# A two-layer-path hybrid mixer step on one core: head sums of the recurrence in runs of five, and an earlier flag that holds back the modulation columns

## The chip, the core and the metric

The kernel runs on one core of one Trainium2 chip. The metric is the time of one execution on the device in microseconds; the medians below are medians of the runs shown. The engines are named as in the profile: PE (matmuls) with PEld (its weight loads), DVE, ACT, POOL, and SP, which only issues transfers.

## What is computed

The reference computes one layer of a diffusion backbone for two groups of tokens: 128 context tokens (`xp`) and 512 latent tokens (`xs`), 640 in all, with 1024 channels. Cut to what matters here:

```python
def trunk_layer(x, cvec, lw, ...):
    mod = jax.nn.silu(cvec) @ lw['w_ada'] + lw['b_ada']        # modulation: six rows of 1024 per group
    sh1, sc1, g1, sh2, sc2, g2 = jnp.split(mod, 6, axis=-1)
    h = rmsnorm(x, lw['norm1_g']) * (1.0 + sc1) + sh1
    mix, ... = token_mixers(h, lw, ...)                        # four gated mixers
    x = x + g1 * mix
    h = rmsnorm(x, lw['norm2_g']) * (1.0 + sc2) + sh2
    x = x + g2 * conv_ffn(h, lw['w_up'], ..., lw['w_down'])

def token_mixers(h, lw, ...):
    proj = h @ lw['w_in']                                      # 13 sections
    y_a = a_b * dwconv3(a_c * a_x, ...)
    y_b, s_f, s_b = hgrn2_bidir(b_q, b_ff, b_fb, b_i, b_g, ...)   # the recurrence, both directions
    y_c = neighbourhood_attention(...)                         # or context_attention
    y_d = chunk_gmlp(d_u, d_v, ...)
    g_a, g_b, g_c, g_d = split(sigmoid(h @ w_gate + b_gate))
    merged = g_a * (y_a @ w_br_a) + g_b * (y_b @ w_br_b) + g_c * (...) + g_d * (...)
    return merged @ lw['w_o'], ...
```

In the recurrence, each of 4 heads of 64 channels has a 64x64 state that decays and is updated along the tokens, forward and backward; the output of a head is normalised by the root mean square of its 64 values (`o * rsqrt(mean(o*o) + EPS)`), scaled and gated.

## The kernel before

Activations lie with channels on the 128 partitions and the 640 tokens along the free dimension, split in a high and a low part (`XH`, `XL`), as is each weight block (`w`, 128x1280 or 128x1024 for each part), so that a product takes three passes of `g` or `m` matmuls. A **main stream** runs through a list of weight blocks: the sections of `w_in` (line 362 inside `gemm_half`, and 933 for two sections with tokens on the partitions), then the gate and branch blocks (still line 362), then the output, up and down products. A block is loaded by SP into a `raw` tile, ACT copies its high part into `w` (lines 310, 323, 148), and the low part is made by DVE (line 324, and 311) or, for some blocks, by a transfer that POOL issues and that accumulates onto `w` (line 148, `w<-raw`).

Beside the main stream run **generators**: `ada_cols` (line 241, modulation columns), `hgrn` (line 445, the recurrence), `gmlp`, `conva`, `attn` (line 729, attention), `g_operands` (line 1011). The main stream counts planned microseconds: each step calls `tick(us)`, which adds to `now` and resumes every generator whose due time has passed; a generator that yields `x` is due again after `x` times its slack (1.3 for `hgrn`). `pe(us)` adds to `now` without resuming any. So the yields set the order in which instructions are written, and a scheduler then fixes the order of each engine from it. The engines work through their orders one instruction at a time.

What the change touches:

- `along(x)` (lines 459 to 469) sums a product of two 128x1280 tiles along the heads: ten matmuls of a 128x128 block with `heads` (128x2, ones for each head's partitions), into one PSUM tile `m`. It is called twice, on tile D and on tile E.
- The tail of `hgrn` (lines 611 to 655). For five blocks of 128 tokens the output `og` is copied out of PSUM, squared (ACT), summed over 64 (line 635, DVE, into `hss`), scaled (line 304, DVE), raised to the power -0.5 (line 305, POOL), and multiplied on (line 610, DVE, `normed`). The product of one block is written behind the sums of the next. Then comes a pause, the last `normed`, the flag `hgrn_y`, a pause `HY` of 4, and five times two transposes (line 648, PE) with their multiply (line 652, DVE). At the end `split_y("D", sg)` and `split_y("E", yt)` (lines 662, 663: a copy by ACT, a subtraction by DVE).
- `ada_cols` makes a modulation column in two halves on DVE: `junk<-H` (or A), then `H<-H` in place (both line 262, 128x1024), each with the sum of its row, and a small `modt` (line 228 or 231). The weights of even columns are loaded to region H, of odd ones to X0 or A, by SP (line 248); the load of column f+2 is written behind the second half of column f. While `hgrn_y` is set and `hgrn_done` is not, it starts no further column.

Two consumers stand behind these on the same engines. The attention works by units: scores on PE (lines 827, 830), bias and maximum on DVE (834, 836), exponential on ACT (837), reciprocal and scaling on DVE (843, 844), three transposes on PE (847), a copy of them to B by DVE (1931) or ACT (1929), the product with the values on PE (864), and its split by ACT and DVE (870, 871). The gate blocks end in a sigmoid on ACT (971; the first one behind the exponentials loads another table), which frees a PSUM tile `g`. Later blocks are of another kind, whose weights `raw` are combined in region H first (line 148, `H<-raw` by ACT, then sums by DVE).

Of the kernel before, what the change touches and what calls it, by code (L numbers as in the profile page):

```python
# [67 lines left out]
def tile_step(ctx: ExitStack, tc: tile.TileContext, a: dict, outs: list, dbg=None):  # L68
# [21 lines left out]
    def pe(us):  # L90
        now[0] += us
# [38 lines left out]
    def pm():  # L130
        return psm.tile([P, 512], F32, tag="m", name=nm("m"))
# [74 lines left out]
    for x in LORD.split():  # L206
        if x[0] == "w":
            i, h = int(x[1]), int(x[2])
# [170 lines left out]
    R = {}  # L379
# [67 lines left out]
    def hgrn():  # L447
# [13 lines left out]
        def along(x):  # L461

            m = pm()
            mv = m[:, 0:20].rearrange("p (r i) -> p i r", r=2)
            for i in range(10):
                mm(mv[:, i, :], x[:, i * P:(i + 1) * P], heads, start=True, stop=True)
                pe(0.22)
                yield 0.5
            return m


# [5 lines left out]
        for j in range(2):  # L477
            vec.tensor_tensor(n2[:, j], k2(j)[:, j], q2(1 - j)[:, 1 - j], ALU.mult)
        dm = yield from along(ksum)

        near_at = hd[:, 1280:1920].rearrange("p (r i t) -> p r i t", r=2, i=10)
# [17 lines left out]
        for l in range(7):  # L499
# [5 lines left out]
            if l == 0:  # L505
                m = yield from along(near)
                vec.copy_predicated(nat, lmask[:, 0, :].unsqueeze(1).to_broadcast([P, 20, 32]), bc(m))
# [101 lines left out]
        def normed(t):  # L609
            vec.tensor_tensor(o3(og, t), o3(og, t), ss[:, 4 * t:4 * t + 4].unsqueeze(2).to_broadcast([P, 4, 64]),  # L610
                              ALU.mult)
# [26 lines left out]
                normed(last)  # L638
            last = t
        R["hgrn_out"] = True  # L640
        yield 2.5
        normed(last)
        R["hgrn_y"] = True
        yield HY
        for t in range(5):
            m = pm()
# [251 lines left out]

    SLACK = {"q": 1.3, "du": 1.4, "ax": 1.0, "cv": 1.1}
    starts = {"q": hgrn, "du": gmlp, "ax": conva, "cv": attn}  # L900

    def in_tile(sec, n, w):
# [1318 lines left out]
```

## Time and profile before

| what | us |
|---|---|
| runs shown | 3496.3, 1024.87, 1024.14 |
| median | 1024.87 |
| the profiled execution's own time | 1023.97 |
| its span in the trace | 1022.1 |
| PE busy, of the span | 1008.3 (99%) |
| DVE busy | 790.1 (77%) |
| ACT busy | 538.6 (53%) |

The granted TensorE clock was 0.998 in the profiled execution. In a row of a timeline stand the start, the duration, the engine, the line, the operation, the tile written and the tiles read, and the number of instructions; brackets behind it give the idle time of the engine just before and what ended it. A tile's name is that of its buffer or region. "DMA to landing" is the time from a load's issue to its arrival. PE's ends are modelled, so starts are compared. A busy PE with an idle gap that has a releaser is a wait; idle time of another engine costs nothing by itself.

### The profile page before, as it was taken

Reading aid. Unit: us, or ns where it says so; the run is one execution under the profiler, and the core shown is the slowest. Engines: PE = TensorE matmul, PEld = TensorE weight load, DVE = VectorE, ACT = ScalarE, POOL = GpSimd, SP = SyncE. Lnnn points to the kernel's source line nnn. Section 1 sums busy time; section 2 is a strip of 40 time slices with the busy share of each in tenths; the row PEclk is TensorE's granted clock in tenths of the full one; section 3 lists DMA queues with packets and bytes.
Section 4 is the critical chain, followed back from the end, with each engine's and each line's share of the span. In section 5 each row is a group of like instructions: output and inputs, shape, how many; then the busy total and the mean of one; then the engine's idle time right before and its main releaser. Section 6 shows DMA issues by size and latency. Waiting matters only on the chain.

```text
span 1022.1 us, 18764 instructions
## 1 busy us (share of the span) xinstructions
PE 1008.3 (99%) x7572; PEld 951.9 (93%) x7572; DVE 790.1 (77%) x1308; ACT 538.6 (53%) x933; POOL 106.5 (10%) x153
## 2 busy tenths in 40 slices
PE   8999999999999999999999999999999999999997
PEld 6899999999899999999998899999999999888886
DVE  6758899769866676767868879998888887796644
ACT  6642343354555444444544567777777776634432
POOL 1000020312100000000010111111112221001101
PEclk9999999999999999999999999999999999999999
DMA  9864433597562413323179584765555669974212
GB/s 354 322 221 127 126 124 114 171 263 216 143 206 79 155 52 104 130 77 104 49 282 349 207 328 112 195 163 150 150 151 149 154 161 271 370 259 146 83 42 103
DMA packets 55926, 177.85 MB, mean 174 GB/s; under 512 B 8192, under 2 KB 14624, under 8 KB 53280
## 3 DMA queue, kind: packets, MB, share of 16 engines
q1 hardware_dynamic: 45008, 140.60, 39.6%
q0 software_dynamic: 10832, 36.06, 14.8%
q8 instruction: 59, 0.97, 0.4%
q14 instruction: 27, 0.22, 0.1%
HBM read 134.93 MB, written 25.46 MB: 157 GB/s over the span
## 4 chain that ended last, share of the span: by engine, by line
PE 91%; DVE 5%; DMA 1%; issue 1%; ACT 1%; POOL 1%; SPq 0%; POOLq 0%; DVEq 0%; ACTq 0%
PE g L1478 19%; PE m L1122 17%; PE g L362 14%; PE g L1813 8%; PE m L1813 6%; PE g L1135 5%; PE m L1478 4%; PE m L1262 3%; PE g L933 2%; PE g L1262 2%; PE m L148 2%; PE g L148 1%; PE m L1473 1%; PE m L526 1%; DMA A<-in_w_ada_dram 1%
## 5 line engine op out<-in xcount | busy, mean ns | idle before, releaser
L362 PE MATMUL g<-XH,w 128*128 128x320 f32 x704 | 171.4, 317 | 0.0
L362 PEld LDWEIGHTS g<-XH,w 128*128 128x128 f32 x704 | 120.6, 188 | 2.4 <-issue 1.2
L362 PE MATMUL g<-XL,w 128*128 128x320 f32 x352 | 108.8, 309 | 0.0
L362 PEld LDWEIGHTS g<-XL,w 128*128 128x128 f32 x352 | 66.3, 188 | 0.0
L311 DVE TENSOR_TENSOR w<-raw,w 128x1024 fp32r<-128x1024 f32 x34 | 41.4, 1221 | 14.9 <-ACT w L310 9.1
L1122 PE MATMUL m<-XH,w 128*128 128x320 f32 x224 | 52.5, 309 | 0.0
L1813 PE MATMUL g<-w,XH 128*128 128x512 f32 (+1 forms) x216 | 50.2, 385 | 0.0
L1813 PEld LDWEIGHTS g<-w,XH 128*128 128x128 f32 x216 | 39.5, 188 | 8.3 <-ACT XH L1772 0.3
L310 ACT ACTIVATE w<-raw 128x1024 fp32r<-128x1024 f32 x34 | 35.7, 1050 | 21.3 <-PE g L1262 10.0
L1813 PE MATMUL g<-w,XL 128*128 128x512 f32 (+1 forms) x180 | 42.4, 386 | 0.0
L148 DVE SCALAR_TENSOR_TENSOR X<-MG,p2t,X 128x641 f32<-128x641 f32 x44 | 38.9, 885 | 4.3 <-ACT X L148 3.4
L148 DVE SCALAR_TENSOR_TENSOR X<-X,p2t,X 128x641 f32<-128x641 f32 x44 | 38.9, 884 | 1.9 <-ACT X L148 1.0
L1813 PEld LDWEIGHTS g<-w,XL 128*128 128x128 f32 x180 | 33.4, 188 | 7.1 <-DVE dt L1828 0.2
L148 ACT ACTIVATE w<-raw 128x1024 fp32r<-128x1024 f32 (+3 forms) x46 | 38.2, 851 | 2.7 <-DMA raw<-in_w_in_dram 1.7
L1478 PE MATMUL g<-XL,w 128*128 128x320 f32 x240 | 38.6, 310 | 0.0
L1478 PE MATMUL g<-XL,C 128*128 128x320 f32 x240 | 38.4, 309 | 0.0
L1122 PEld LDWEIGHTS m<-XH,w 128*128 128x128 f32 x224 | 38.3, 188 | 0.0
L1478 PEld LDWEIGHTS g<-XL,w 128*128 128x128 f32 x240 | 36.0, 188 | 0.5 <-ACT MG L148 0.3
L1813 PE MATMUL m<-w,XH 128*128 128x512 f32 (+1 forms) x156 | 36.4, 381 | 0.0
L1478 PEld LDWEIGHTS g<-XL,C 128*128 128x128 f32 x240 | 35.9, 188 | 0.4 <-ACT MG L148 0.4
L1122 PE MATMUL m<-XL,w 128*128 128x320 f32 x112 | 34.6, 309 | 0.0
L1813 PEld LDWEIGHTS m<-w,XH 128*128 128x128 f32 x156 | 28.5, 188 | 5.6
(549 smaller groups left out, 2751.9 us busy)
## 6 DMA issues: line engine op xcount, KB each, us to landing
raw<-in_w_up_dram SPq DMA_DIRECT2D x30, 512.0 KB, 4.9
raw<-in_w_gp_dram SPq DMA_DIRECT2D x21, 640.0 KB, 4.0
raw<-in_w_down_dram SPq DMA_DIRECT2D x22, 512.0 KB, 4.0
raw<-in_w_in_dram SPq DMA_DIRECT2D x19, 512.0 KB, 4.2
H<-in_w_adt_dram SPq DMA_DIRECT2D x16, 512.0 KB, 4.5
actd<-X POOLq DMA_DIRECT2D x22, 320.5 KB, 5.4
X<-in_w_adt_dram SPq DMA_DIRECT2D x10, 512.0 KB, 4.0
upd<-XL SPq DMA_DIRECT2D x4, 1280.0 KB, 6.4
```

The source lines that it names most:

```text
L148: r = f(*args, **kw)
L310: act(w[0], raw, AF.Copy)
L311: vec.tensor_tensor(w[1], raw, w[0].bitcast(F32), ALU.subtract)
L362: mm(o, w[:, h, k0 + k, :], r(k)[:, s], start=(k == 0 and i == 0), stop=(k == kt - 1 and i == 2))
L526: mm(m[W * g:W * g + W, (i - s0) * W:(i - s0 + 1) * W], lhs, rhs, start=True, stop=True, tile_position=(64 * par, W * g))
L933: mm(o, x(kx)[:, ts], w[:, h, k, :], start=(kx == 0 and i == 0), stop=(kx == 7 and i == 2))
L1122: mm(o, w[:, k, :], x[:, k, :], start=(first and k == 0 and j == 0), stop=(k == 3 and j == 2), skip_group_check=True)
L1135: mm(pb[:, c, 0:HC], w[:, h + k, :], y[:, x, k, s], start=(k == 0 and j == 0), stop=(k == 1 and j == 2))
L1262: mm(m, mh[k // 2][:, hx, k % 2, t * P:(t + 1) * P], wo[q][:, hw, k % 2, :], start=(k == 0 and i == 0), stop=(k == 7 and i == 2))
L1473: mm(o, w[:, k, :], x[:, k, :], start=(first and not part and k == 0 and j == 0), stop=(part == 1 and k == 3), skip_group_check=True)
L1478: z = mm(o, w[:, k, :], x[:, k, :], start=(first and k == 0 and j == 0), stop=(k == 3 and j == 2), skip_group_check=True)
L1813: mm(ps, sl[k][hx][:, t * P:(t + 1) * P], w[:, hw, k, c0:c1], start=first, stop=end and (last or nh == 1 and t == 4 and kk_ == 7))
```

## The change

In `along` the generator yields after the fifth and the tenth matmul, 3.5 planned us each, in place of 0.5 after every one. At the end of the recurrence the pause of 2.5 before the last `normed` is split in 0.5 and 2, and the flag `hgrn_y`, which stops further modulation columns, is set between them: 2 planned us sooner, ahead of the last `normed`.

```diff
             for i in range(10):
                 mm(mv[:, i, :], x[:, i * P:(i + 1) * P], heads, start=True, stop=True)
                 pe(0.22)
-                yield 0.5
+                if i % 5 == 4:
+                    yield 3.5
             return m
...
         R["hgrn_out"] = True
-        yield 2.5
+        yield 0.5
+        R["hgrn_y"] = True
+        yield 2
         normed(last)
-        R["hgrn_y"] = True
         yield HY
```

Since the yields set the order, more rows move than the diff shows. On PE the ten sums of a run now stand in two groups of five (before, mostly one by one), and the recurrence's later matmuls stand three to nine matmuls of the main stream earlier. Three places show what else moves. In the rows below, the numbers in names are those of buffers and differ between the two programs, and the brackets name what an instruction waits for: an engine's counter, DMAHW (a transfer of SP's) or DMASW (one of POOL's).

On DVE, the end of the recurrence, from the last reductions (`hss<-B`) to the first multiply behind the transposes. `MG<-MG,hss` is `normed`, `E<-X,E` is a subtraction of another branch, A and H hold columns' weights. Before:

```order
L262 SCALAR_TENSOR_TENSOR junk_2568,ar_2569<-A_2326,S_94_1047 128x1024 [waits DMAHW7_49]
L304 TENSOR_SCALAR hss_2506<-hss_2506 128x4 [waits DVE_49]
L635 TENSOR_REDUCE hss_2506<-B_795 128x4 [waits Activation_49]
L610 TENSOR_TENSOR MG_113_1229<-MG_113_1229,hss_2506 128x256 [waits Pool_49]
L304 TENSOR_SCALAR hss_2506<-hss_2506 128x4 [waits DVE_49]
L262 SCALAR_TENSOR_TENSOR A_2326,ar_2569<-A_2326,S_94_1047 128x1024
L635 TENSOR_REDUCE hss_2506<-B_795 128x4 [waits Activation_49]
L610 TENSOR_TENSOR MG_113_1229<-MG_113_1229,hss_2506 128x256 [waits Pool_49]
L304 TENSOR_SCALAR hss_2506<-hss_2506 128x4 [waits DVE_49]
L228 TENSOR_SCALAR modt<-ar_2569,cst 128x2
L610 TENSOR_TENSOR MG_113_1229<-MG_113_1229,hss_2506 128x256 [waits Pool_49]
L663 TENSOR_TENSOR E_2728<-X_126_1318,E_2728 128x1280 [waits PE_49,Activation_49]
```

And now:

```order
L304 TENSOR_SCALAR hss_2491<-hss_2491 128x4 [waits DVE_49]
L262 SCALAR_TENSOR_TENSOR junk_2577,ar_2578<-A_2337,S_94_1047 128x1024 [waits DMAHW7_49]
L636 TENSOR_REDUCE hss_2491<-B_795 128x4 [waits Activation_49]
L611 TENSOR_TENSOR MG_113_1231<-MG_113_1231,hss_2491 128x256 [waits Pool_49]
L304 TENSOR_SCALAR hss_2491<-hss_2491 128x4 [waits DVE_49]
L262 SCALAR_TENSOR_TENSOR A_2337,ar_2578<-A_2337,S_94_1047 128x1024
L611 TENSOR_TENSOR MG_113_1231<-MG_113_1231,hss_2491 128x256 [waits Pool_49]
L228 TENSOR_SCALAR modt<-ar_2578,cst 128x2 [waits DVE_49]
L665 TENSOR_TENSOR E_2722<-X_124_1314,E_2722 128x1280 [waits PE_49,Activation_49]
L262 SCALAR_TENSOR_TENSOR junk_2731,ar_2732<-H_2520,S_94_1047 128x1024 [waits DMAHW5_49]
L262 SCALAR_TENSOR_TENSOR H_2520,ar_2732<-H_2520,S_94_1047 128x1024 [waits DVE_49]
L654 SCALAR_TENSOR_TENSOR MG_113_1231<-m_2667,cst,MG_113_1231 128x128 [waits PE_49]
```

Of the five ways from a scaling (line 304) over POOL's power to the `normed` that waits for it, a column half now stands in three (two are in these rows), before in one; the column on H stands ahead of the first multiply (line 652 before, 654 now) in both.

On DVE, about six units into the attention; C's row ends one unit's product, the pair of `X<-m,B` starts the next, and the copy to B is one that PE's products wait for. Before:

```order
L871 TENSOR_TENSOR C_2790<-m_3142,C_2790 128x8x16 [waits Activation_49]
L707 SCALAR_TENSOR_TENSOR MG_261_2890<-MG_261_2890,cst 128x511 [waits DVE_49]
L834 TENSOR_TENSOR X_243_2788<-m_3152,B_2789 128x384 [waits PE_49,Pool_49]
L834 TENSOR_TENSOR X_243_2788<-m_3154,B_2789 128x384 [waits PE_49,Pool_49]
L836 TENSOR_REDUCE ast_2850<-X_243_2788 128x1 [waits DVE_49] x2
L262 SCALAR_TENSOR_TENSOR junk_3168,ar_3169<-A_2326,S_94_1047 128x1024 [waits DMAHW1_49]
L1931 COPY B_2789<-m_3173 128x384 [waits PE_49]
L262 SCALAR_TENSOR_TENSOR A_2326,ar_3169<-A_2326,S_94_1047 128x1024 [waits DVE_49]
```

And now:

```order
L873 TENSOR_TENSOR C_2790<-m_3145,C_2790 128x8x16 [waits Activation_49]
L262 SCALAR_TENSOR_TENSOR junk_3213,ar_3214<-H_3087,S_94_1047 128x1024 [waits DMAHW5_49]
L836 TENSOR_TENSOR X_243_2788<-m_3155,B_2789 128x384 [waits PE_49,Pool_49]
L836 TENSOR_TENSOR X_243_2788<-m_3157,B_2789 128x384 [waits PE_49,Pool_49]
L838 TENSOR_REDUCE ast_2851<-X_243_2788 128x1 [waits DVE_49] x2
L262 SCALAR_TENSOR_TENSOR A_2337,ar_3137<-A_2337,S_94_1047 128x1024
L1933 COPY B_2789<-m_3175 128x384 [waits PE_49]
```

The first half of the column on H, which waits for a load of SP's, now stands ahead of this unit and its copy; before it stood nineteen rows behind C's row, behind the next unit's maxima.

On ACT, at the end of the attention; `gt` is the first sigmoid with its table load, `w` are weight blocks of the main stream, A is `split_y`'s copy. Before:

```order
L323 ACTIVATE w_3463<-raw_3218 128x1280 [waits DMAHW6_49,DMASW5_49,PE_49]
L662 ACTIVATE A_3460<-MG_261_2890 128x1280 [waits DVE_49]
L148 ACTIVATE w_3463<-raw_3218 128x1280
L870 ACTIVATE C_2790<-m_3481 128x8x16 [waits PE_49]
L1929 ACTIVATE B_2789<-m_3525 128x384 [waits PE_49]
L837 ACTIVATE X_243_2788,ast_2850<-X_243_2788,ast_2850 128x384 [waits DVE_49,Activation_49] x2
L870 ACTIVATE C_2790<-m_3552 128x8x16 [waits PE_49]
L971 ACT_TABLE_LOAD
L971 ACTIVATE gt_3575<-g_3471,cst 128x640 [waits PE_49]
L1929 ACTIVATE B_2789<-m_3590 128x384 [waits DVE_49,PE_49]
```

And now:

```order
L323 ACTIVATE w_3463<-raw_3221 128x1280 [waits DMAHW6_49,DMASW5_49,PE_49]
L148 ACTIVATE w_3463<-raw_3221 128x1280
L664 ACTIVATE A_3460<-MG_261_2890 128x1280 [waits DVE_49]
L872 ACTIVATE C_2790<-m_3481 128x8x16 [waits PE_49]
L1931 ACTIVATE B_2789<-m_3525 128x384 [waits PE_49]
L839 ACTIVATE X_243_2788,ast_2851<-X_243_2788,ast_2851 128x384 [waits DVE_49,Activation_49] x2
L872 ACTIVATE C_2790<-m_3552 128x8x16 [waits PE_49]
L148 ACTIVATE H_3693<-raw_3468 128x256 [waits DMAHW2_49]
L973 ACT_TABLE_LOAD
L973 ACTIVATE gt_3575<-g_3471,cst 128x640 [waits PE_49]
L1931 ACTIVATE B_2789<-m_3590 128x384 [waits PE_49]
```

The copy `H<-raw`, which waits for a load, now stands ahead of the table load and the sigmoid; before it stood eight rows behind the sigmoid. The second copy into `w` and the copy to A have changed places.

## The prediction

> Line numbers are those of the kernel before; in the changed file lines behind the change are one or two higher.
>
> **What bounds the kernel.** I read the page's busy times and its chain that ended last, then the windows by stage.
>
> ```profile
> span 1022.1 us, 18764 instructions
> ...
> PE 1008.3 (99%) x7572; PEld 951.9 (93%) x7572; DVE 790.1 (77%) x1308; ACT 538.6 (53%) x933; POOL 106.5 (10%) x153
> ...
> PE 91%; DVE 5%; DMA 1%; issue 1%; ACT 1%; POOL 1%; SPq 0%; POOLq 0%; DVEq 0%; ACTq 0%
> ```
>
> TensorE is busy in 99% of the span and carries 91% of the last chain. A change that leaves its work alone can win only the little time in which it waits, and loses whatever new wait it makes. So I look for waits of PE. In the windows the columns are start:end, length, then busy time and (instructions) of PE, PEld, DVE, ACT, POOL, then clock, DMA share and GB/s.
>
> ```profile
> 190.00:210.00 20.00, 18.98 (x133) 18.54 (x132) 12.70 (x31) 10.16 (x17) 7.50 (x8) 1.00 0.72 188
> ...
> 250.00:270.00 20.00, 19.48 (x143) 16.94 (x142) 18.23 (x48) 7.89 (x18) 6.15 (x8) 1.00 0.72 192
> ...
> 290.00:311.00 21.00, 21.00 (x145) 21.00 (x144) 9.88 (x10) 6.82 (x9) 0.00 (x0) 1.00 0.62 196
> ```
>
> From 70 to 311 us, where the change moves anything, PE is idle for 1.0 us in the stretch that holds the recurrence's last transposes and 0.5 us in the attention's. From 290 us DVE is half idle, so a delay of DVE is made up there, but one of PE is not.
>
> **Part 1: the sums along heads in runs of five.** Twenty matmuls stay twenty, each of two records; only their neighbours change. A lone one and two in a row read:
>
> ```profile
> 92.03 0.28 PE L466 MATMUL m<-heads,E 128*128 128x2 f32 x2
> ...
> 83.88 0.50 PE L466 MATMUL m<-heads,D 128*128 128x2 f32 x4
> ```
>
> Alone 0.28 us, two in a row 0.25 each: 20 x 0.25 to 20 x 0.28 is 5.0 to 5.6 us, so grouping lies between -0.6 and nothing; I take 0. What hangs on the second run comes earlier on PE by three to nine matmuls of the main stream.
>
> **Part 2: the wait ahead of the transposes goes.** On DVE the group of five waits, and the rows behind it:
>
> ```profile
> DVE MG L610 <- POOL hss L305: 4.3, 5, 1.1
> ...
> 195.90 1.49 DVE L663 TENSOR_TENSOR E<-X,E 128x1280 fp32r<-128x1280 f32 x1
> 197.31 1.22 DVE L262 SCALAR_TENSOR_TENSOR junk<-H,S 128x1024 bf16<-128x1024 f32 x1
> ...
> 200.16 0.61 DVE L652 SCALAR_TENSOR_TENSOR MG<-m,cst,MG 128x128 f32<-128x128 f32 x2
> ...
> 198.97 0.31 PE L362 MATMUL g<-XL,w 128*128 128x320 f32 x1
> 199.12 0.31 PE L362 MATMUL g<-XH,w 128*128 128x320 f32 x1
> ...
> 200.56 0.33 PE L648 MATMUL m<-cst,MG 128*128 128x128 f32 x1 [1.02 <-DVE MG L652]
> ```
>
> The second transpose group waits for L652, which stands behind a modulation column (two passes from 197.31). The earlier flag does not take that column away: the changed order still has both its passes ahead of the first L652. What helps is the row order before it: DVE goes five times from L304 over POOL's power L305 to L610 and idles through 4.3 us of this; a column half of 1.2 us stood in one of the five ways, now it stands in three. Two more covered at about 0.9 each (4.3 over five) make 1.7, and the H half that now comes between two scalings somewhat more; L652 can start some 2 us sooner, at 198.2. PE came there at 200.56 - 1.02 = 199.5; its transposes stand six main matmuls earlier in the changed order, 6 x 0.15 (198.97 to 199.12) = 0.9, so at 198.6. That is just enough; the gain lies between 0.5 and 1.0, and I take 1.0. **Term: -1.0.**
>
> **Part 3: a modulation column now blocks DVE (the main loss).** The same shift of the planned times puts the next even column one attention unit earlier in DVE's order: `junk<-H` with its wait for a load now stands directly behind L871, ahead of the unit's L834 pair, its L836 pair, the other column's second half and the copy L1931 that PE's next group L864 needs. Before it stood one unit later. The load's place on SP is the same. Rows of DVE, PE and POOL, and the two loads' issue and landing:
>
> ```profile
> 242.20 0.28 DVE L871 TENSOR_TENSOR C<-m,C 128x128 fp32r<-128x128 f32 x1
> ...
> 243.06 1.01 DVE L834 TENSOR_TENSOR X<-m,B 128x384 f32<-128x384 f32 x2
> 243.99 0.99 DVE L836 TENSOR_REDUCE ast<-X 128x1 f32<-128x384 f32 x2
> 244.91 1.57 DVE L262 SCALAR_TENSOR_TENSOR junk<-A,S 128x1024 bf16<-128x1024 f32 x1
> ...
> 246.41 0.55 DVE L1931 COPY B<-m 128x384 f32<-128x384 f32 x1
> ...
> 252.79 1.21 DVE L262 SCALAR_TENSOR_TENSOR junk<-H,S 128x1024 bf16<-128x1024 f32 x1
> 253.94 0.07 DVE L262 DVE_READ_ACCUMULATOR junk<-H,S 128x1 f32 x1
> ...
> 248.12 0.66 PE L864 MATMUL m<-B,X 128*64 128x128 f32 x8
> ...
> 254.40 0.55 PE L847 MATMUL m<-cst,X 128*128 128x128 f32 x3 [0.25 <-DVE X L844]
> ...
> 240.71 0.99 POOL L148 DMA_DIRECT2D w<-raw  x1 [3.37 <-ACT w L148]
> ...
> L248 SPq DMA_DIRECT2D H<-in_w_adt_dram x1: 383/383/383, 241.5 to 241.5; - x1
> ...
> DMA to landing us min/median/max: 9.6/9.6/9.6
> ...
> L248 SPq DMA_DIRECT2D A<-in_w_adt_dram x1: 333/333/333, 231.8 to 231.8; - x1
> ...
> DMA to landing us min/median/max: 7.9/7.9/7.9
> ```
>
> H's load is issued at 241.5 and lands 9.6 us later, at 251.1, beside POOL's transfer of 240.71. DVE waited for none of it, since it came to `junk<-H` at 252.79. In the changed order DVE comes to it at about 242 and stands idle until the landing. When is that? If what releases the load (SP's queue ahead of it, POOL, ACT) follows PE's gain of 1.0, it is issued at 240.5 and lands at 250.1; if not, at 251.1; if it takes the 7.9 us of A's load, at 248.4. I take 249.6, between the first and the last and nearer the H row, which is the same load. Then come junk 1.15 (252.79 to 253.94), L834 0.93 (243.06 to 243.99), L836 0.92 (243.99 to 244.91), A's half 1.15 (as the junk) and the copy 0.55: 4.7 us, done at 254.3. PE stood there at 248.12, so it is 6.2 us late (between 5.0 and 7.7); part 2's gain is used up in this, since the end of the wait is set by the landing. Late next is L844, for which PE waits at L847: seven rows of DVE that before lay beside PE's work now follow the copy, 0.7 more than the 0.25 shown; the 0.5 of idle in 250:270 goes otherwise, as groups behind it find DVE ahead by one column half. **Term: 6.2 + 0.7 - 0.5 = +6.4, part 2 included.** The column before it has moved in the same way, and its load changed places with one on SP:
>
> ```profile
> L248 SPq DMA_DIRECT2D H<-in_w_adt_dram x1: 530/530/530, 220.1 to 220.1; - x1
> ...
> DMA to landing us min/median/max: 11.9/11.9/11.9
> ```
>
> It landed at 232.0 and, issued about a microsecond later, would land near 233, a little behind DVE's turn; PE may wait some half a microsecond for that, which the later landing of 249.6 swallows. What waits behind `junk<-H` on DVE is the attention alone; SP's and POOL's queues are not held, except that H's buffer comes free later for the next column, which has no due time near.
>
> **Part 4: a weight block's copy now blocks ACT.** `H<-raw` (L148, 128x256) waits for a load and moved from behind the three L1047 to ahead of the table load and the sigmoid L971, whose end frees the PSUM tile for PE's next gate group. Rows of ACT, POOL, PE, and the load:
>
> ```profile
> 272.15 1.25 ACT L662 ACTIVATE A<-MG 128x1280 fp32r<-128x1280 f32 x1
> 273.30 1.26 ACT L148 ACTIVATE w<-raw 128x1280 fp32r<-128x1280 f32 x1
> ...
> 280.66 1.28 ACT L971 ACT_TABLE_LOAD   x1
> 281.95 0.80 ACT L971 ACTIVATE gt<-g,cst 128x640 f32<-128x640 f32 x1
> ...
> 289.81 0.40 ACT L148 ACTIVATE H<-raw 128x256 fp32r<-128x256 f32 x1
> ...
> 274.86 0.89 POOL L148 DMA_DIRECT2D w<-raw  x1 [5.51 <-PE m L847]
> ...
> 283.65 0.30 PE L362 MATMUL g<-XH,w 128*128 128x320 f32 x1
> ...
> L1059 SPq DMA_DIRECT2D raw<-in_w_gp_dram x1: 328/328/328, 281.6 to 281.6; - x1
> ...
> DMA to landing us min/median/max: 4.0/4.0/4.0
> ```
>
> The load is issued at 281.6, when POOL's transfer of 274.86 is through, and lands at 285.6; before, ACT came to it at 289.81. That transfer follows ACT's w of 273.30, which in the changed order no longer stands behind L662: 1.2 us sooner, so a landing at 284.4. Then 0.40 + 1.28 + 0.80: the sigmoid ends at 286.9, and PE wants the tile at 283.65. **Term: +3.2** (4.4 if the load comes no sooner). All of this moves with PE's delay from part 3, so it adds.
>
> The Trainium skill ("ScalarE: Activation LUTs", What ACT_TABLE_LOAD costs) adds a drain of about 1.38 us to each switch of table. By that, a switch on the path would make the term 4.6 and the sum 1.4 more. The trace has the sigmoid start 281.95 - 280.66 = 1.29 us behind the load's start, which leaves no room for it, and the row decides.
>
> **Sum.** 0 + 6.4 + 3.2 = +9.6 us on the profiled execution's 1023.97: 1033.6. The median of the runs is 1024.87, 0.9 above that execution; against it the time would be 1034.5.
>
> **Rivals.**
> - *H's load is in time, only ACT stalls.* For it: A's load took 7.9, and DVE may come late. Against it: before, the load landed only 1.7 us ahead of its use, and the use moves 10 us. Time: -1.0 - 0.5 + 3.2 = +1.7, 1025.7. Chance 0.12.
> - *ACT's copy finds its data, only DVE stalls.* It needs a landing 3 us sooner still. Time: +6.4, 1030.4. Chance 0.12.
> - *The other side: SP's queue runs ahead.* Both blocked rows wait for loads that SP issues in order, behind loads that wait for POOL's transfers. If those transfers start earlier than I think, since ACT's w no longer waits behind other rows, both loads land before their use. That decides once H's load is issued 8 us sooner, at 233. For it: part 4's 1.2 us; against it: POOL's transfers of this stretch are released by ACT's w, which follows PE. Time: -1.0 - 0.5, 1022.5. Chance 0.08.
> - *The DVE stall goes on.* The late evictions of the main stream hold PSUM tiles, and PE waits again behind 256 us, by at most another column of two halves, 2.4 us, besides a landing at 251.1 (+1.5): 1037.5. Chance 0.10.
>
> **Numbers.** The forecast of two stalls has 0.58. Predicted: 1033.6. The range takes in the first two rivals and most of the fourth, 1025.0 to 1037.0; outside lie the third (0.08) and some 0.08 of the tails. Its own range for two stalls is 1031 to 1036. Two per cent, about what a measurement of this kernel can tell from no change, is 20.5 us: none of the cases reaches it. Faster by over 2%: 0.01; within: 0.97; slower by over 2%: 0.02.
>
> **What would show it.** Right: L648's wait is gone near 200 us; DVE idles 6 to 9 us at one `junk<-H` released by a DMA, near 242 to 250; PE then waits about 6 us at L864 and 3 us at one L362 released by ACT's sigmoid, with `H<-raw` just before the table load; PE's busy time stays at 1008. Wrong: a heads run that takes over 0.3 us a matmul (part 1); the 1.0 still there (part 2); no idle time of DVE at `junk<-H` (part 3); the table load without a wait ahead of it (part 4). The forecast falls altogether if PE's idle time from 190 to 311 us stays under 2 us.

## The result: 1.5% slower, beyond the range

The changed kernel took 1039.81 us (median of 4 runs, 1036.79 to 1041.45) where the kernel before took 1024.53; the ratio is 1.0147, with a 95% interval of 1.0117 to 1.0177. Forecast were 1033.6, between 1025.0 and 1037.0. The ratio leaves out the one run of 3496.3 us. The profiled execution is the slowest of the four (1041.45); its span is 1039.7 us, 17.6 more than the 1022.1 before.

The first lines of the page after, to be read against those shown of before:

```profile
span 1039.7 us, 18763 instructions
...
PE 1016.4 (98%) x7572; PEld 958.4 (92%) x7572; DVE 790.1 (76%) x1308; ACT 539.2 (52%) x933; POOL 107.9 (10%) x153
...
PE 89%; DVE 4%; DMA 4%; issue 1%; ACT 1%; POOL 1%; SPq 0%; POOLq 0%; DVEq 0%; ACTq 0%
```

The work of DVE and ACT is what it was. PE has the same 7572 matmuls and is busy 8.1 us longer, which no wait explains; 4.8 of these lie at the two stalls shown next. The last chain now has 4% of transfers. PE's waits between 70 and 330 us (line waited at, releaser, sum, times, longest):

```profile
PE m L866 <- DVE B L1933: 7.8, 1, 7.8
PE g L362 <- ACT gt L973: 3.3, 1, 3.3
PE m L650 <- DVE MG L654: 0.6, 1, 0.6
PE m L527 <- issue: 0.2, 1, 0.2
```

Both forecast stalls are there. DVE's, and the rows behind it (lines are one or two higher than before):

```profile
244.08 0.28 DVE L873 TENSOR_TENSOR C<-m,C 128x128 fp32r<-128x128 f32 x1
253.07 1.22 DVE L262 SCALAR_TENSOR_TENSOR junk<-H,S 128x1024 bf16<-128x1024 f32 x1 [8.71 <-DMA H<-in_w_adt_dram]
...
254.22 1.02 DVE L836 TENSOR_TENSOR X<-m,B 128x384 f32<-128x384 f32 x2
255.16 1.00 DVE L838 TENSOR_REDUCE ast<-X 128x1 f32<-128x384 f32 x2
256.07 1.29 DVE L262 SCALAR_TENSOR_TENSOR A<-A,S 128x1024 f32<-128x1024 f32 x1
...
257.29 0.55 DVE L1933 COPY B<-m 128x384 f32<-128x384 f32 x1
```

DVE stands idle for 8.7 us until the column's weights land at 253.07, and then does four things before the copy that PE waits for. On ACT the copy into H waits for its load ahead of the table load:

```profile
291.27 0.28 ACT L872 ACTIVATE C<-m 128x128 fp32r<-128x128 f32 x1 [1.51 <-PE m L866]
295.42 0.42 ACT L148 ACTIVATE H<-raw 128x256 fp32r<-128x256 f32 x1 [3.87 <-DMA raw<-in_w_gp_dram]
295.85 1.28 ACT L973 ACT_TABLE_LOAD   x1
297.15 0.80 ACT L973 ACTIVATE gt<-g,cst 128x640 f32<-128x640 f32 x1
```

What the forecast does not have is in the eighth column of the windows (start:end, length, busy time of PE, PEld, DVE, ACT, POOL, then **the granted clock**, DMA share, GB/s):

```profile
246.00:250.00 4.00, 4.00 (x29) 3.80 (x27) 0.00 (x0) 0.00 (x0) 0.00 (x0) 1.00 0.98 243
250.00:254.00 4.00, 0.08 (x1) 0.00 (x0) 0.93 (x1) 0.00 (x0) 0.00 (x0) 0.87 0.35 76
254.00:258.00 4.00, 0.11 (x2) 0.11 (x4) 4.00 (x11) 2.21 (x6) 1.41 (x2) 0.50 0.40 149
258.00:262.00 4.00, 4.00 (x24) 3.27 (x25) 4.00 (x10) 1.96 (x3) 1.22 (x2) 0.50 0.53 154
262.00:266.00 4.00, 4.00 (x25) 4.00 (x24) 3.74 (x9) 1.31 (x4) 1.19 (x2) 0.85 0.74 143
266.00:270.00 4.00, 4.00 (x31) 3.65 (x29) 3.31 (x11) 1.25 (x2) 0.00 (x0) 1.00 0.47 164
292.00:296.00 4.00, 2.72 (x21) 2.45 (x19) 3.14 (x3) 0.56 (x2) 0.00 (x0) 1.00 0.47 164
296.00:300.00 4.00, 2.00 (x7) 2.01 (x8) 1.31 (x2) 3.99 (x5) 0.00 (x0) 0.67 0.01 2
300.00:304.00 4.00, 4.00 (x20) 3.67 (x21) 2.55 (x4) 1.80 (x2) 0.87 (x1) 0.50 0.15 29
304.00:308.00 4.00, 4.00 (x31) 3.83 (x29) 2.89 (x4) 2.60 (x3) 0.00 (x0) 0.98 1.06 288
```

While PE waits, its clock falls to half, and when the wait is over PE goes on at half: 20 to 24 matmuls in 4 us where 31 were done at full clock. The matmuls themselves show where it ends (PE, start and duration; 262.99 is the last slow one):

```profile
262.19 0.47 PE L362 MATMUL g<-XL,w 128*128 128x320 f32 x1
262.45 0.73 PE L362 MATMUL g<-XH,w 128*128 128x320 f32 x2
262.99 0.41 PE L362 MATMUL g<-XL,w 128*128 128x320 f32 x1
...
263.96 0.31 PE L362 MATMUL g<-XL,w 128*128 128x320 f32 x1
264.11 0.46 PE L362 MATMUL g<-XH,w 128*128 128x320 f32 x2
264.40 0.31 PE L362 MATMUL g<-XL,w 128*128 128x320 f32 x1
```

Three of them take 0.80 us (262.19 to 262.99) at half clock and 0.44 us (263.96 to 264.40) at full.

**Where the 17.6 us lie.** The n-th matmul of the main stream (1392 of lines 362 and 933) is the same work in both traces, so the difference of its starts is what has been lost up to there.

| main matmul | before | after | lost so far | lost since the row above |
|---|---|---|---|---|
| first | 49.31 | 49.38 | 0.07 | 0.07 |
| 354th, behind both runs of sums | 102.45 | 102.83 | 0.38 | 0.3 |
| 512th | 129.20 | 130.35 | 1.15 | 0.8 |
| 1051st, ahead of the first stall | 246.27 | 248.15 | 1.88 | 0.7 |
| 1201st, ahead of the second | 281.48 | 292.39 | 10.91 | 9.0 |
| 1231st, behind it | 287.18 | 304.40 | 17.22 | 6.3 |
| last | 310.90 | 328.11 | 17.21 | 0.0 |

The remaining 0.4 us of the 17.6 lie behind the last main matmul. The second stall cost 6.3 us although PE waited 3.3.

### The profile page after: what moved, and what is told of

Same layout as the page of the kernel before. It is cut to its first block, busy times and chain, and to the rows that moved or that the text cites. A ratio compares the mean times of both kernels' runs of the same rounds, so it can differ in the third digit from the quotient of the medians.

```text
span 1039.7 us, 18763 instructions
## 1 busy us (share of the span) xinstructions
PE 1016.4 (98%) x7572; PEld 958.4 (92%) x7572; DVE 790.1 (76%) x1308; ACT 539.2 (52%) x933; POOL 107.9 (10%) x153
## 4 chain that ended last, share of the span: by engine, by line
PE 89%; DVE 4%; DMA 4%; issue 1%; ACT 1%; POOL 1%; SPq 0%; POOLq 0%; DVEq 0%; ACTq 0%
PE g L1480 19%; PE m L1124 17%; PE g L362 14%; PE g L1815 8%; PE m L1815 5%; PE g L1137 5%; PE m L1480 4%; PE m L1264 3%; PE g L935 2%; PE g L1264 2%; PE m L148 2%; PE g L148 1%; PE m L527 1%; PE m L1475 1%; DMA H<-in_w_adt_dram 1%
## 5 line engine op out<-in xcount | busy, mean ns | idle before, releaser
L362 PEld LDWEIGHTS g<-XH,w 128*128 128x128 f32 x704 | 122.7, 191 | 6.3 <-ACT gt L973 3.5
L323 ACT ACTIVATE w<-raw 128x1024 fp32r<-128x1024 f32 (+1 forms) x22 | 24.3, 1103 | 20.4 <-issue 7.8
```

Source lines behind the costliest of these rows:

```text
L323: high = lambda: act(w[:, 0], raw, AF.Copy)
L362: mm(o, w[:, h, k0 + k, :], r(k)[:, s], start=(k == 0 and i == 0), stop=(k == kt - 1 and i == 2))
```

## The experiments

Two theories stood. The first, call it **columns and clock**: the change matters only through the planned times of the last modulation columns, which put one row on DVE and one on ACT ahead of work that PE needs; the waits cost their length, and more through the clock. The rival: the recurrence's moved rows, or the grouped sums themselves, cost the time. The planner's own counter speaks for the first. Its value when each column starts, as the program is written:

| column | before | whole change | sums alone | flag alone |
|---|---|---|---|---|
| 35 | 175.25 | 174.43 | 174.43 | 174.43 |
| 36 | 181.96 | 180.01 | 180.01 | 180.01 |
| 37 | 188.67 | 185.90 | 185.90 | 185.90 |
| 38 | 195.38 | 192.61 | 192.61 | 192.61 |

A shift of 0.8 grows to 2.8, since a column starts at the next tick, and the counter moves in jumps there; and each part alone gives the same as both. Eleven runs follow. Each is compared with the kernel before on the same chip (1024.1 to 1024.6 us), by the ratio of the runs.

### Each part alone

```diff
             for i in range(10):
                 ...
-                yield 0.5
+                if i % 5 == 4:
+                    yield 3.5
```

> The changed recurrence sums alone (runs of five), with the pause and the flag as before. Theory: each part of the change by itself brings modulation columns 36 to 39 forward by the same 2.8 planned us, and that is what sets both stalls; so this kernel shows both (PE waits of about 7.8 us at the copy to B and 3.3 us at the sigmoid, each followed by a stretch at clock 0.5) and takes 1036 to 1041 us, as the whole change does. Rival: the stalls come from the earlier flag; then this kernel is at 1024 to 1027 us.

Measured: 1040.07 us, ratio 1.0147 (1.0121 to 1.0173). In its profile PE waits 7.7 us at the copy to B, 3.2 at the sigmoid and 2.2 ahead of the transposes. The clock is at half for 6.83 us behind the first and for 3.41 behind the last, but not behind the wait at the sigmoid; this part of the expectation failed:

```profile
298.79 0.42 PE L362 MATMUL g<-XH,w 128*128 128x320 f32 x1 [3.17 <-ACT gt L972]
...
298.00:302.00 4.00, 3.21 (x25) 3.02 (x26) 2.52 (x3) 4.00 (x5) 0.00 (x0) 1.00 0.00 0
```

```diff
-        yield 2.5
+        yield 0.5
+        R["hgrn_y"] = True
+        yield 2
         normed(last)
-        R["hgrn_y"] = True
```

> The earlier flag alone, the head sums one by one as before. Theory: both stalls again, since the columns are planned as early as in the whole change; 1035 to 1040 us, about 1.2 us less than the whole change, because lone sums cost 0.14 us and grouped ones 0.22. Rival (the grouped sums are the cause, by moving the recurrence): within 1 us of the kernel before.

Measured: 1035.32 us, ratio 1.0117 (1.0088 to 1.0146). PE's waits are 3.7 and 3.4 us, each with 3.41 us of half clock. That this is faster than the sums alone does not show a cost of grouping: here the load of column 38's weights took 6.9 us, there 9.7. Both parts bring both stalls by themselves, so neither is "the" cause; what they share is the columns' time.

### The columns alone, and the columns put back

The kernel before, with nothing changed but a pause in `ada_cols`:

```diff
             if f == 35:
-                yield 4
+                yield 3.2
```

> The kernel before with neither part of the change; only the pause ahead of column 35 is 3.2 instead of 4 planned us, which brings columns 35 to 39 forward and puts the two blocked rows on DVE and ACT where the change puts them. Theory (the columns alone set the loss): both stalls and the clock at 0.5 behind them, 1033 to 1039 us. Rival (the recurrence's moved rows are needed too): within 3 us of the kernel before.

Measured: 1038.33 us, ratio 1.0121 (1.0101 to 1.0141). DVE's row shows the same stall, with the recurrence as it was:

```profile
252.35 1.23 DVE L262 SCALAR_TENSOR_TENSOR junk<-H,S 128x1024 bf16<-128x1024 f32 x1 [10.01 <-DMA H<-in_w_adt_dram]
```

And the other way, the whole change with the columns' times restored from column 36 on (181.96, 188.67, 195.38):

```diff
             if f == 35:
-                yield 4
+                yield 4.8
```

> The whole change, and the pause ahead of column 35 made 4.8 instead of 4 planned us, so that columns 35 to 39 fall due as in the kernel before; on DVE and ACT the two blocked rows stand again where they stood before. Theory: no stall, no stretch at clock 0.5; left are the grouped sums (+1.2) and small waits against the shorter wait ahead of the transposes: 1024 to 1027 us. Rival (the recurrence's own earlier rows, not the columns, make the loss): 1033 us or more.

Measured: 1025.53 us, ratio 1.0014 (1.0005 to 1.0023). No wait is left but small ones (0.6 us at the most from 70 to 330 us), and the clock stays at 1.0 where both stalls were:

```profile
250.00:270.00 20.00, 19.89 (x155) 17.17 (x154) 18.23 (x46) 9.00 (x17) 5.57 (x8) 1.00 0.72 180
...
290.00:311.00 21.00, 21.00 (x145) 21.00 (x144) 10.71 (x13) 8.02 (x10) 0.87 (x1) 1.00 0.67 219
```

This settles the first theory's main point: with the columns in place, 14 of the 15 us are gone; without the change but with early columns, 12 (by the ratio) to 14 (by the medians) are lost.

> The earlier flag, the head sums one by one, and the pause ahead of column 35 made 4.8, so that both blocked rows stand where they stood before. Theory: beside the paced whole change (1025.5) this saves the cost of grouping the sums, 1.2 us by the starts of the matmuls: 1024.0 to 1024.6 us, no clear difference from the kernel before. Rival (the 1.4 us that the paced whole change lost come from the other moved rows): 1025 to 1026 us.

Its edit is the flag's with the pause of 4.8. Measured: 1024.46 us, ratio 1.0001 (0.9992 to 1.0009). So what the paced whole change still loses, about 1.3 us by the ratios (with some 1.2 either way), goes with the first part of the change; the earlier flag with the columns in place neither wins nor loses. The expected number came out, but not for its reason: by the starts of the matmuls the grouped sums themselves cost 0.3 us, not 1.2, as the last part shows.

### One stall at a time

```diff
         for b, x in zip(gw[p_, "br"], r):
-            oact(b[:, 0:2], x[:, 8:10], AF.Copy)
+            z = oact(b[:, 0:2], x[:, 8:10], AF.Copy)
+            if p_ == 0:
+                tc.keep_in_program_order(z)
```

> The whole change, with ACT's copy into H held in program order, so that it stands behind the table load and two sigmoids; the column's early half on DVE stays. Theory: the wait of 3.3 us at the sigmoid and the stretch at clock 0.5 behind it go (about 5.7 us together), the first stall stays: 1032 to 1036 us. Rival (the clock falls for another reason than PE's wait): only 3.3 us less than the whole change, 1036 to 1037.

Measured: 1032.73 us, ratio 1.0078 (1.0061 to 1.0095). In its profile nothing is lost from the 1201st to the 1231st main matmul, where the whole change lost 6.3 us; the other wait, 7.9 us, stood. By ratios, (1.0147 - 1.0078) x 1024 = 7.1 us went with a wait of 3.3, but with some 3.5 either way this alone does not rule out the rival.

### The clock

Is it the wait that slows the clock? Then work that keeps PE busy during the wait must keep the clock. The first attempt put 30 matmuls on zeros, into the sum that the main stream had open, ahead of the products of the first stall (in the pinned kernel):

```diff
+    def fill(n):
+        for _ in range(n):
+            tc.keep_in_program_order(nc.tensor.matmul(at_["o"][0:30, 0:P], scv[:, 0, 2:32], cst[:, 0:P],
+                                                      start=False, stop=False, skip_group_check=True))
...
+            if u == 6:
+                fill(30)
             if u > 0:
                 s3(u - 2)
```

> The whole change with the copy into H pinned (so one stall is left, at the copy to B), and 30 more matmuls on TensorE just ahead of the blocked products, that add products with zeros to the gate's sum and leave it as it is; they fill most of the 7.9 us wait and need nothing. Theory (clock follows TensorE's idleness): the products start at the same time, the clock stays at 1.0 there, and the time is 2 to 2.7 us below that of the pinned kernel's 1032.7: 1030 to 1031. Rival (PE is slow behind the stall because DVE is behind): no change, 1032.5 to 1033, or longer by what the added matmuls do not hide.

Measured: 1035.39 us, ratio 1.0107 (1.0093 to 1.0120), so slower than the pinned kernel: the expectation on the time failed. The rows tell why. PE, at the place of the wait:

```profile
249.93 6.74 PE L177 MATMUL g<-cst,scv 128*30 128x128 f32 x60
256.60 0.66 PE L873 MATMUL m<-B,X 128*64 128x128 f32 x8
...
258.65 0.31 PE L369 MATMUL g<-XH,w 128*128 128x320 f32 x1
261.29 0.90 PE L856 MATMUL m<-cst,X 128*128 128x128 f32 x3 [2.33 <-DVE X L853]
```

The products ran at full clock (0.66 us for eight, where the whole change took 1.12), but three main matmuls later PE met DVE, which was still working off what the stall had piled up, and waited 2.3 us more; the added rows had also moved this group forward on PE. This second wait brought 3.41 us of half clock of its own, from 260.6 us on. So this run does not tell the two theories apart on the total; it suggests that behind the first stall DVE's backlog covers a part of the half clock, as a PE at full speed waits there instead.

The second stall has no such backlog. Eleven matmuls on zeros ahead of the last three of the branch product in front of it:

```diff
+        if at_["n"] == 1:
+            gemm_half(pb[:, 0, 0:HC], 0, w, 8, range(2), 2, *yr)
+            gemm_half(pb[:, 1, 0:HC], 1, w, 8, range(1), 2, *yr)
+            fill(pb[:, 1, 0:HC], 11)
+            gemm_half(pb[:, 1, 0:HC], 1, w, 8, range(1, 2), 2, *yr)
```

> The whole change, and eleven more matmuls (2.5 us, products with zeros added to the branch's sum, which they leave as it is) ahead of the last three of the branch product that precedes the wait at the sigmoid; the order of everything else on TensorE is the same. They need nothing and delay only work whose reader waits for the sigmoid. Theory (TensorE's clock falls when it idles through most of a window of 3.4 us): the blocked group starts at the same time, its wait falls from 3.3 to about 0.8 us, the clock stays at 1.0 there, and the time is 2.5 to 3.2 us below the whole change's. Rival (PE is slow there for another reason): the same time as the whole change, within 0.7 us.

> The whole change again, beside the filled kernel on the same chip: 1037 to 1041 us, as before; waits of 7.8 and 3.3 us, each with a stretch at clock 0.5 that begins and ends at a boundary of a grid of 3.413 us, so that the time differs from run to run by 2 us or more.

Measured: filled 1038.90 us, ratio 1.0139 (1.0122 to 1.0156); the whole change 1037.56, ratio 1.0124 (1.0109 to 1.0139). On the total the expectation failed again, but at the place itself the rows are as expected. PE and then the windows of the filled kernel:

```profile
293.89 2.59 PE L177 MATMUL g<-cst,scv 128*30 128x128 f32 x22
296.41 0.71 PE L367 MATMUL g<-E,w 128*128 128x320 f32 x3
297.51 0.41 PE L367 MATMUL g<-XH,w 128*128 128x320 f32 x1 [0.39 <-ACT gt L978]
```

```profile
296.00:298.00 2.00, 1.61 (x11) 1.15 (x9) 0.41 (x1) 1.99 (x4) 0.00 (x0) 1.00 0.00 0
298.00:300.00 2.00, 2.00 (x16) 2.00 (x15) 0.97 (x1) 2.00 (x2) 0.00 (x0) 1.00 0.00 0
```

The wait falls to 0.4 and the clock stays at 1.0. From the 1201st to the 1231st main matmul the filled kernel loses 3.4 us (10.59 to 13.97), no more than the wait; the whole change lost 6.3, and in its second profile 5.1 (6.72 to 11.84). So the clock made 1.7 to 2.9 us of the second stall. Profiles without any added work say the same, since nearly the same wait at the sigmoid is followed by none, one or two windows of 3.41 us at half clock:

| profile | PE's wait | half clock behind it | lost from the 1201st to the 1231st |
|---|---|---|---|
| sums alone | 3.2 | none | 3.4 |
| early columns | 3.1 | 3.41 | 4.9 |
| flag alone | 3.4 | 3.41 | 5.2 |
| whole change, second profile | 3.3 | 3.41 | 5.1 |
| whole change, first profile | 3.3 | 6.83 | 6.3 |

The total of the filled kernel hid this, because the first stall differed by more in the profiled executions: in the second profile of the whole change the column's load took 6.8 us in place of 9.8.

```profile
249.88 1.22 DVE L262 SCALAR_TENSOR_TENSOR junk<-H,S 128x1024 bf16<-128x1024 f32 x1 [4.50 <-DMA H<-in_w_adt_dram]
...
DMA to landing us min/median/max: 6.8/6.8/6.8
...
PE m L866 <- DVE B L1933: 4.2, 1, 4.2
```

PE's wait was 4.2 there, in the filled kernel 8.1. To take this out, the last pair leaves out the two sums of column 38 on DVE (`if f != 38:` ahead of them), so that only the second stall can occur, without and with the same eleven matmuls.

> The whole change, but the two sums of modulation column 38 on DVE are left out (the column gets the sums of column 37), its load and its planned times stay. So the first stall cannot occur, and the second stands as in the whole change. Theory: 1.4 us for the recurrence's moved rows, 3.3 us of waiting at the sigmoid, and 1.7 to 3 us for the windows at clock 0.5 behind it: 1030 to 1032 us. Rival (no loss beyond the wait): 1029.

> The same kernel (column 38's sums left out), and eleven more matmuls (2.5 us, products with zeros added) ahead of the last three of the branch product in front of the wait; nothing else on TensorE changes its place. Theory: the blocked group starts at the same time, but at clock 1.0: 1.7 to 3 us below the kernel without them, 1028 to 1029.5. Rival: no difference, within 0.5 us.

Measured: 1031.84 us, ratio 1.0077 (1.0065 to 1.0089), and 1032.10, ratio 1.0070 (1.0056 to 1.0085): no difference on the total, as the rival had it; a third miss. At the place it is again 4.9 against 3.3 us (3.06 to 7.94, 5.46 to 8.77). But both kernels wait 2.6 us at an attention group ahead of it, and in the profile of the filled one this wait brought 3.41 us of half clock, in the other it did not. So no run gives the time of the whole kernel with the waits and without the half clock; its price is read at the place alone.

## Why the prediction was wrong, step by step

**The step that failed: "All of this moves with PE's delay from part 3, so it adds", and with it the sum itself.** The terms counted each wait once, and let PE run on at full clock behind it. There is no term for the clock, and no rival with one. Measured are 9.0 and 6.3 us at the two stalls, where PE's waits are 7.8 and 3.3. In the second the difference of 3.0 is the half clock. In the first, matmuls at half clock make 2.5 us by their starts, and 1.3 us that PE lost at L847 before are gone.

The sum was 9.6 us and the profiled execution lost 17.6. Of the 8.0 missing, 5.5 are the half clock at the two stalls. The rest are a first wait longer by 1.6 (7.8 in place of 6.2) against 1.5 less at L847 than the sum had, 1.9 lost ahead of the stalls, where the sum has nothing, and 0.4 behind. Without the half clock the execution of 1041.45 would have come to about 1036, inside the range; this is an estimate from these rows, and a low one, since DVE's backlog would have taken a part of the gain.

The Trainium skill ("TensorE: Matmul & The Clock Gate", What's actually happening) says that TensorE's clock halves after an idle window of about 3.4 us, and that the windows run freely. The trace agrees on the length and on the lack of a fixed place: the half-clock stretches of the first profile after last 10.24 and 6.83 us, 3 and 2 times 3.413, and where the first of them begins differs from profile to profile (252.96 in the first of the whole change, 254.29 in the second). The same page of the Trainium skill, section "HAM oscillation — how this bites in real kernels" puts the bound at idle gaps of over some 3.4 us; here a wait of 3.3 us was enough, and in the profile of the sums alone one of 2.2 us, while one of 3.2 us in the same profile was not. What differs between these waits is where the windows' boundaries fall. Counted in steps of 3.413 us from the half-clock stretches, the wait of 3.3 us took up 2.6 us of one window, and that of 2.2 lay in one window as a whole; the one of 3.2 was divided, 1.8 and 1.3. No sharp bound follows, since 1.7 us of a window were enough in the kernel with 30 added matmuls.

Point by point, in the order of the forecast:

- *Grouping the sums costs nothing* (between -0.6 and 0): nearly right; it cost 0.3 us, all of it in the run on D. I read durations, which overlap; the starts tell. Main matmuls start 0.15 us apart without a sum. A lone sum pushes the next one back by 0.14, and the one behind that by 0.08 more; five in a row (ten records) push them back by 1.03 and 0.08, again 0.22 for each sum. The 0.14 against 0.22 of the expectation for the flag alone left out the second step. Before, and now:

```profile
91.89 0.31 PE L362 MATMUL g<-XH,w 128*128 128x320 f32 x1
92.03 0.28 PE L466 MATMUL m<-heads,E 128*128 128x2 f32 x2
92.17 0.39 PE L362 MATMUL g<-XH,w 128*128 128x320 f32 x1
92.40 0.31 PE L362 MATMUL g<-XL,w 128*128 128x320 f32 x1
...
92.83 1.17 PE L466 MATMUL m<-heads,E 128*128 128x2 f32 x10
93.86 0.39 PE L362 MATMUL g<-XH,w 128*128 128x320 f32 x1
94.09 0.31 PE L362 MATMUL g<-XL,w 128*128 128x320 f32 x1
```

From the 294th to the 354th main matmul, around the run on E, PE takes 11.00 us before and 11.03 now; around the run on D, 191st to 251st, 9.57 and 9.85. The 0.8 us that the table has between the 354th and the 512th arise behind the sums, and they differ between executions: the second profile of the whole change has 0.2 there and that of the sums alone 0.0. Their cause stays open.

- *The wait ahead of the transposes goes, -1.0*: it fell from 1.0 to 0.6. DVE's idle time behind POOL's power fell from 4.3 to 3.1 us only: POOL's power, 1.01 us otherwise, takes 1.91 beside a column half of DVE, which stands in three of the five ways now and stood in one before. Two rows of now:

```profile
189.59 1.01 POOL L305 TENSOR_TENSOR hss<-hss,neghalf 128x4 f32<-128x4 f32 x1 [0.62 <-DVE hss L304]
191.21 1.91 POOL L305 TENSOR_TENSOR hss<-hss,neghalf 128x4 f32<-128x4 f32 x1 [0.62 <-DVE hss L304]
```

- *The earlier flag does not take the column away*: right; with the columns in place the flag alone is worth nothing (1.0001).
- *Part 3, +6.4*: the mechanism was right, at the place named; the size was 9.0. DVE idled 8.7 us where 6 to 9 were forecast. The landing was at 253.1, not 249.6: the load was issued at 243.3, not 240.5, since PE was late by 1.9 instead of early by 1.0, and took 9.8 us, which I had shortened toward the 7.9 of another load. The end the prediction kept for the range, 251.1 with 9.6, was nearer.
- *Part 4, +3.2*: PE waited 3.3. The size of the wait was right to 0.1, the drain of the table load was rightly left out, the half clock behind it was missing.
- *The rivals*: the nearest was that the DVE stall goes on (1037.5); it had the wrong reason. Both single-stall rivals and the one on the other side did not occur.
- *What would show it*: "PE's busy time stays at 1008" was the test that told the error; it rose to 1016.4, and 4.8 of the 8.1 us lie at the two stalls, where matmuls at half clock count as busy.

What stays open: how far the waits alone, without the clock, would have gone over the whole kernel (three attempts met other waits); what makes the losses ahead of the stalls, beyond the 0.3 of the sums; and why the same load takes 6.8 us in one execution and 9.8 in another.

## What to carry to other kernels

When a change makes the bounding TensorE wait, price the wait, and then look at the granted clock behind it: here a wait of 3.1 to 3.4 us cost 3.4 without half clock and 4.9 to 6.3 with it. In a kernel whose order comes from a planner, look for rows with a wait for a load that have moved ahead of other work on an in-order engine, and undo the planned time rather than the change: one pause of 4.8 in place of 4 took back 14 of 15 us. For the cost of small matmuls between others read starts, not durations, and over a whole run: the first matmul behind a small one does not carry all of its cost.

## What the runs showed of the hardware that was not expected

The half clock begins and ends on a grid of windows of 3.413 us that has no fixed place in the kernel. A wait of 3.2 us brought none of it in one profile, and one of 2.2 us in the same profile did. The load that the first stall waits for landed 6.8 to 9.9 us after its issue. The profiles of one kernel differ in these two things; they fit, but do not prove, the spread of the stalled kernels, 2 to 7 us from run to run (1034.29 to 1039.82 for the early columns alone), where the paced one's ten runs lie within 1.9 and the kernel before stays within 1 to 2 on a chip.
